# Latent attention: the queries of a head pair made one pair ahead, in output tiles not yet written

## The chip, the core and the metric

The kernel runs on one core of a Trainium2 chip. The core has five engines, each with an instruction stream of its own: TensorE (PE in the profile) multiplies matrices, its weight loads are shown apart as PEld, VectorE (DVE) and ScalarE (ACT) do elementwise work, GpSimd (POOL) helps out, and SyncE (SP) issues transfers from the memory of the chip (HBM). ScalarE issues some transfers too; the profile shows those as ACTq. On-chip data lives in SBUF (128 partitions), sums of matrix products in the banks of PSUM. The metric is the device time of one execution in microseconds (us), lower is better.

## What is computed

Two layers of a decoder trunk with three parallel branches (Mamba-2, latent attention, gated DeltaNet), a merge, an output projection and a feed-forward network, for one sequence of 512 tokens with 1024 channels, in float32. The branch that matters here is the latent attention. Cut to it, the reference is:

```python
def mla_mixer(cq, ckv, k_rope, cos, sin, q_norm_g, w_uq, kv_norm_g, w_ukv):
    H = MLA_HEADS                                  # 8 heads
    q = (rmsnorm(cq, q_norm_g) @ w_uq).reshape(Bsz, S, H, 128 + 64)
    q_nope, q_pe = jnp.split(q, [MLA_NOPE], axis=-1)
    q_pe = apply_rope(q_pe, cos, sin)
    kv = (rmsnorm(ckv, kv_norm_g) @ w_ukv).reshape(Bsz, S, H, 128 + 128)
    k_nope, v = jnp.split(kv, [MLA_NOPE], axis=-1)
    k_pe = apply_rope(k_rope, cos, sin)            # one key for all heads
    sc = (q_nope @ k_nope.T + q_pe @ k_pe.T) * scale, causal
    pr = softmax(sc)
    o = pr @ v
```

Here `cq` has 512 latent channels and `ckv` 256. Each head's query has 128 plain channels and 64 rotary ones.

## The kernel before

**Precision.** Every dense product is made of three matmuls of split numbers, high times high, low times high and high times low (L181, L182, L183 in `mm3`). Weights come from HBM into a raw tile (`wraw`, two buffers), ScalarE rounds the high half (`whi`, L159) and VectorE subtracts it to get the low half (`wlo`, L160); four buffers each of `whi` and `wlo`. The query weights have a split of their own, in four pieces (L552, L553 on ScalarE, L554, L555 on VectorE), because the plain and the rotary channels of a pair of heads are laid apart.

**Order of work.** The program text is a sequence of operations. A planner (the tile framework's scheduler) turns it into one fixed order of instructions for each engine: it goes by the place of an operation in the text, lifted where the text says `high_priority`, by its own costs, and by when buffers come free. So TensorE interleaves work of several steps, and a step's place in the text sets where it may appear, not exactly where. Buffers are rings of tiles with a common tag; a new tile waits until the last reader of the old one is done. What matters here: two raw weight tiles, four accumulator banks (`acc`), three small banks (`sm`) and one output bank (`yt`) in PSUM, eight tiles `mix`, and three tiles each for the plain queries and keys (`qh`, `ql`, `kh`, `kl`).

**Latent attention.** A layer first makes small projections and the latents `cq` and `ck`, with their norms (function `latent`, L500 and L260/L261). Then a loop goes over four pairs of heads, `hp` 0 to 3. For each pair it makes

- the queries: weights (L541 to L556), 36 matmuls of 128x512 (`dense_F`), then `qh`/`ql` for the two heads (L568, L569) and the rotary part `qp` for both (L575). The rotary part goes through `rope`: four transfers issued by ScalarE that exchange its halves (L513), three operations of VectorE (L515 to L517), then two more transfers that swap the heads (L580) and the copies into `qps` and `qpl` (L584, L585, and L586, which reads what the transfers brought). `qpl` is half zero: that half is set once for all pairs (L536);
- the keys: 12 matmuls, `kh`/`kl` (in `head_tiles`, written by `split_act`, L256 and L257);
- the values: 24 matmuls of 128x256, evacuated in eight pieces, by L256 and L257 too. Pairs 0 and 2 have tiles for them; pair 1 writes them into the output tiles `y6` and `y7`, pair 3 into the latent tiles `cq0` and `cq1`, which are not needed any more or not yet;
- for each of the two heads: scores for four blocks of 128 queries (L617 to L619 plain, L620 and L621 rotary, L622 the mask), row maximum (L626, VectorE), exponential (L629, ScalarE), reciprocal and scaling (L630, L631, VectorE), transposes (L639), and the product with the values (L655 to L657), split into the output tiles `y0` to `y7`.

After pair 0 the loop also makes the step sizes of another branch (`step_sizes`). Layer 1 does the loop at about 66 to 195 us of the span, layer 2 at about 1226 to 1358 us. Then a next stage (`ssd_group`) follows, and the planner lets its first matmuls fill gaps in the last pairs.

Of the kernel before, what the change touches and what calls it, by code (L numbers as in the profile page):

```python
# [11 lines left out]
F32R = mybir.dt.float32r  # L12
# [3 lines left out]
ALU = mybir.AluOpType  # L16
# [4 lines left out]
P = 128  # L21
S = 512
# [37 lines left out]
def hybrid_kernel(ctx, tc, a, out, depth=2, taps=None):  # L60
# [4 lines left out]
    def mk(pl, shape, dt, tag, bufs=None):  # L65
        return pl.tile(shape, dt, tag=tag, name=f"{tag}_{next(uid)}", bufs=bufs)
# [5 lines left out]
    def f32(ap):  # L72
        return ap.bitcast(F32)
# [180 lines left out]
    def split_act(hi, lo, src):  # L254
        with tc.high_priority(30):
            act.copy(hi, src)  # L256
            dve.tensor_tensor(lo, src, f32(hi), ALU.subtract)  # L257
# [78 lines left out]
    for ly in range(depth):  # L336
# [34 lines left out]
        ps = sm_bank()  # L371
# [159 lines left out]
        for x in pts:  # L531
            pool.memset(f32(x[:, :P]), 0.0)

        qpl = [mk(ml, [P, S], F32R, f"qpl{j}") for j in range(2)]
        for j in range(2):
            pool.memset(f32(qpl[j][64 * (1 - j) : 64 * (1 - j) + 64]), 0.0)  # L536

        scale = (128 + 64) ** -0.5
        yh, yl = [None] * KD, [None] * KD
        for hp in range(4):  # L540
            def q_weights():  # L541
                for k0 in (0, 2):
                    raw = mk(wp, [P, 768], F32, "wraw", 2)
                    sync.dma_start(raw.rearrange("p (k n) -> p k n", k=2),
                                   a["mla_w_uq"][ly][k0 * P : (k0 + 2) * P, hp * 384 : (hp + 1) * 384].rearrange("(k p) n -> p k n", p=P))
                    for k in range(2):
                        rv = raw[:, k * 384 : (k + 1) * 384].rearrange("p (h n) -> p h n", h=2)
                        hi = mk(wp, [P, 384], F32R, "whi")
# [6 lines left out]
                        dve.tensor_tensor(pv(lo), rv[:, :, P:], f32(pv(hi)), ALU.subtract)  # L555
# [4 lines left out]
            def head_tiles(pss, nm, c=None):  # L560
                res = []
                for ps in pss:
                    hi = mk(ml, [P, S], F32R, nm + "h", 3)
                    lo = mk(ml, [P, S], F32R, nm + "l", 3)
                    if c is None:
                        split_act(hi, lo, ps)
                    else:
                        act.mul(hi, ps, c)  # L568
                        dve.scalar_tensor_tensor(lo, ps, c, f32(hi), ALU.mult, ALU.subtract)  # L569
                    res.append((hi, lo))  # L570
                return res

            qs = head_tiles(pq, "q", scale)
            qp = mk(ml, [P, S], F32, "qp")
            act.mul(qp, pp, scale)  # L575
            qr = rope(qp)

            qd = mk(lp, [P, S], F32, "mix", 8)
            for i in range(2):
                act.dma_start(qd[64 * i : 64 * i + 64], qr[64 * (1 - i) : 64 * (1 - i) + 64])  # L580
            qps = [mk(ml, [P, S], F32R, f"qps{j}") for j in range(2)]
            for j in range(2):
                half, other = (slice(64 * i, 64 * i + 64) for i in (j, 1 - j))
                act.copy(qps[j][half], qr[half])  # L584
                dve.tensor_tensor(qpl[j][half], qr[half], f32(qps[j][half]), ALU.subtract)  # L585
                act.copy(qps[j][other], qd[other])  # L586
            wkv = list(weights(a["mla_w_ukv"][ly], hp * 512, 512, 256))
            with tc.high_priority(30):
                ks = head_tiles(dense_F(wkv, [slice(0, P), slice(256, 256 + P)], 256, ckh, ckl), "k")

            vs = []
            for j in range(2):
                if hp % 2 == 0:
                    v2 = [mk(ml, [P, S], F32R, nm, 2) for nm in ("vh", "vl")]
                elif hp == 1:
                    v2 = [mk(lp, [P, S], F32R, f"y{e}{6 + j}") for e in "hl"]
                else:
                    v2 = [mk(ml, [P, S], F32R, f"cq{e}{j}") for e in "hl"]
                vs.append([x.rearrange("p (t n) -> p t n", t=T) for x in v2])

            def ev(t, ps):
                for j in range(2):
                    split_act(*(x[:, t, :] for x in vs[j]), ps[:, j * P : (j + 1) * P])

            vcols = lambda w: w.rearrange("p (h n) -> p h n", h=2)[:, :, P:]
            dense_T(wkv, 256, 256, ckh, ckl, ev, vcols)

            for j in range(2):
                qh, ql = qs[j]
                kh, kl = ks[j]  # L610
                pn = []
                for t in range(T):
                    n = max(256, (t + 1) * P)
                    tok = slice(t * P, (t + 1) * P)
                    ps = sm_bank()
                    o = ps[:, :n]
                    pe.matmul(o, qh[:, tok], kh[:, :n], start=True, stop=False)  # L617
                    pe.matmul(o, qh[:, tok], kl[:, :n], start=False, stop=False)
                    pe.matmul(o, ql[:, tok], kh[:, :n], start=False, stop=False)  # L619
                    pe.matmul(o, qps[j][:, tok], kps[:, :n], start=False, stop=False)  # L620
# [8 lines left out]
                    act.activation(pt_[:, :n], o, AF.Exp, bias=mx, accum_out=sm)  # L629
                    dve.reciprocal(sm, sm)  # L630
                    dve.tensor_scalar(pt_[:, :n], pt_[:, :n], sm, None, ALU.mult)  # L631
                    pn.append(pt_)
                po = y_bank()
                for kbs in ((0,), (1,), (3, 2)):
                    ps = sm_bank()
                    n = 0
                    for kb in kbs:
                        for t in range(kb, T):
                            pe.transpose(ps[:, n : n + P], pn[t][:, kb * P : (kb + 1) * P], ident)  # L639
                            n += P  # L640
                    if len(kbs) == 1:
                        th = mk(lp, [P, n], F32R, "mix", 8)
                        tl = mk(lp, [P, n], F32R, "mix", 8)
                        split_act(th, tl, ps[:, :n])
                        parts = [(kbs[0], kbs[0] * P, 0)]
                    else:

                        th, tl = pts
                        split_act(th[:, P:], tl[:, P:], ps[:, :n])
                        parts = [(2, 2 * P, 2 * P), (3, 2 * P, 0)]  # L650
                    for kb, c0, c in parts:
                        v_h, v_l = (x[:, kb, :] for x in vs[j])
                        o = po[:, c0:]
                        w = S - c0
                        pe.matmul(o, v_h, th[:, c : c + w], start=kb == 0, stop=False)  # L655
                        pe.matmul(o, v_h, tl[:, c : c + w], start=False, stop=False)
                        pe.matmul(o, v_l, th[:, c : c + w], start=False, stop=kb == T - 1)  # L657
                yh[2 * hp + j], yl[2 * hp + j] = (mk(lp, [P, S], F32R, f"y{e}{2 * hp + j}") for e in "hl")
                split_act(yh[2 * hp + j], yl[2 * hp + j], po)
                tap(f"oT{2 * hp + j}", f32(yh[2 * hp + j]))  # L660
            if hp == 0:
                dec, ndec, beta, dtq, dsk, g24 = step_sizes()
        mp.close()
# [621 lines left out]
```

## Time and profile before

| | |
|---|---|
| time, median of 3 runs | 2350.89 us (2350.47 to 2352.99) |
| time of the profiled execution | 2350.16 us |
| its span | 2348.4 us |
| granted clock of TensorE, mean | 0.999 |
| TensorE busy | 2307.8 us, 98% |
| VectorE busy | 1607.3 us, 68% |
| ScalarE busy | 1154.4 us, 49% |
| GpSimd busy | 58.5 us, 2% |
| moved by transfers | 215.16 MB, 92 GB/s over the span |

How to read the lines that follow. In a timeline a row is: start (us), duration (us), engine, line and operation, output <- input by the program's names, the tile's size, the count, and in brackets how long the engine was idle before it and what ended that idle time. In a list of waits a row is: engine, output and line of the waiting instruction, what it waited for, then the total in us, the number of times, and the longest. Matmuls overlap, so the time that one costs is the distance of two starts, not its duration. Line numbers are those of the kernel before.

### The profile page before, as it was taken

The numbers are of one execution on the slowest core, as the hardware profiler recorded it, in microseconds if no ns is written. First come the engines' busy times: TensorE is split into PE (matmuls) and PEld (weight loads), VectorE is DVE, ScalarE is ACT, GpSimd is POOL, SyncE is SP. The second block draws the span as 40 slices with busy tenths as digits, with TensorE's granted clock in tenths as the row PEclk, the third lists the DMA queues.
The fourth block names the chain that finished last, engine by engine and source line by source line (L and its number), as shares of the span: only waits on it lengthen the run. The fifth ranks groups of instructions, "written<-read, shape, count | busy, mean of one in ns | idle before, by whom it ended". The sixth has DMA issues, their size and how long they took to land.

```text
span 2348.4 us, 32069 instructions
## 1 busy us (share of the span) xinstructions
PE 2307.8 (98%) x11972; PEld 1896.2 (81%) x11972; DVE 1607.3 (68%) x3184; ACT 1154.4 (49%) x2305; POOL 58.5 (2%) x76
## 2 busy tenths in 40 slices
PE   8999999999999999999999999999999999999998
PEld 7787788888887888888887887888887878888886
DVE  6776756775675458767757777667766645677668
ACT  5655434533453345545656553444334534555545
POOL 0000000000000000000000000000000000000000
PEclk9999999999999999999999999999999999999999
DMA  4322232252222443233132222323422224333231
GB/s 131 91 64 72 65 97 70 79 149 73 73 63 72 143 150 102 72 125 117 46 100 78 73 72 70 93 65 106 117 81 66 62 81 161 126 111 105 90 108 45
DMA packets 194172, 215.16 MB, mean 92 GB/s; under 512 B 32352, under 2 KB 153696, under 8 KB 194016
## 3 DMA queue, kind: packets, MB, share of 16 engines
q1 hardware_dynamic: 190496, 207.87, 29.1%
q10 hardware_dynamic: 3520, 5.25, 0.9%
q8 instruction: 94, 1.54, 0.3%
q14 instruction: 62, 0.51, 0.1%
HBM read 200.50 MB, written 7.34 MB: 89 GB/s over the span
## 4 chain that ended last, share of the span: by engine, by line
PE 90%; DVE 5%; DMA 2%; ACT 1%; POOL 1%; issue 1%; SPq 0%; ACTq 0%; DVEq 0%; POOLq 0%
PE acc L181 23%; PE acc L182 23%; PE acc L183 23%; PE sm L183 2%; PE sm L181 2%; PE sm L182 2%; PE sm L735 1%; DVE wlo L160 1%; PE sm L639 1%; PE yt L182 1%; PE yt L181 1%; PE yt L183 1%; PE sm L1000 1%; PE sm L296 1%; PE sm L461 1%
## 5 line engine op out<-in xcount | busy, mean ns | idle before, releaser
L160 DVE TENSOR_TENSOR wlo<-wraw,whi 128x512 fp32r<-128x512 f32 x552 | 377.9, 688 | 401.8 <-ACT whi L159 391.8
L159 ACT CAST whi<-wraw 128x512 fp32r<-128x512 f32 x552 | 341.9, 621 | 623.6 <-PE acc L182 407.9
L181 PE MATMUL acc<-xh,whi 128*128 128x512 f32 (+1 forms) x1184 | 462.0, 391 | 0.0
L182 PE MATMUL acc<-xl,whi 128*128 128x512 f32 (+1 forms) x1184 | 459.4, 388 | 0.0
L183 PE MATMUL acc<-xh,wlo 128*128 128x512 f32 (+1 forms) x1184 | 459.0, 388 | 0.0
L182 PEld LDWEIGHTS acc<-xl,whi 128*128 128x128 f32 x1184 | 223.0, 188 | 42.5 <-issue 1.0
L183 PEld LDWEIGHTS acc<-xh,wlo 128*128 128x128 f32 x1184 | 222.9, 188 | 41.8 <-issue 0.5
L181 PEld LDWEIGHTS acc<-xh,whi 128*128 128x128 f32 x1184 | 222.8, 189 | 41.7 <-issue 0.5
L181 PE MATMUL acc<-yh,whi 128*128 128x512 f32 x384 | 153.1, 402 | 0.0
L182 PE MATMUL acc<-yl,whi 128*128 128x512 f32 x384 | 152.3, 397 | 0.0
L183 PE MATMUL acc<-yh,wlo 128*128 128x512 f32 x384 | 151.4, 394 | 0.0
L183 PE MATMUL acc<-whi,xl 128*128 128x512 f32 (+1 forms) x384 | 144.0, 375 | 0.0
L181 PE MATMUL acc<-whi,xh 128*128 128x512 f32 (+1 forms) x384 | 143.9, 376 | 0.0
L182 PE MATMUL acc<-wlo,xh 128*128 128x512 f32 (+1 forms) x384 | 143.4, 373 | 0.0
L676 DVE SCALAR_TENSOR_TENSOR cva<-acc,pc,cva 128x511 f32<-128x511 f32 (+2 forms) x168 | 120.2, 743 | 16.7 <-ACT cva L672 9.5
L159 ACT CAST whi<-wr 128x512 fp32r<-128x512 f32 x128 | 79.5, 621 | 68.3 <-PE acc L183 32.7
L181 PE MATMUL acc<-whi,yh 128*128 128x512 f32 x256 | 99.7, 390 | 0.0
L183 PE MATMUL acc<-whi,yl 128*128 128x512 f32 x256 | 99.7, 389 | 0.0
L182 PE MATMUL acc<-wlo,yh 128*128 128x512 f32 x256 | 99.6, 389 | 0.0
L160 DVE TENSOR_TENSOR wlo<-wr,whi 128x512 fp32r<-128x512 f32 x128 | 85.8, 685 | 12.6 <-ACT whi L159 12.1
L182 PEld LDWEIGHTS acc<-yl,whi 128*128 128x128 f32 x384 | 72.2, 188 | 16.1 <-issue 1.9
L181 PEld LDWEIGHTS acc<-yh,whi 128*128 128x128 f32 x384 | 71.6, 188 | 16.8 <-ACT yh L260 2.3
(409 smaller groups left out, 4597.9 us busy)
## 6 DMA issues: line engine op xcount, KB each, us to landing
wraw<-in_w_in_dram SPq DMA_DIRECT2D x148, 512.0 KB, 3.6
wraw<-in_w_up_dram SPq DMA_DIRECT2D x64, 512.0 KB, 3.7
wr<-in_w_down_dram SPq DMA_DIRECT2D x32, 1024.0 KB, 5.0
wraw<-in_w_mla_out_dram SPq DMA_DIRECT2D x16, 512.0 KB, 3.4
wraw<-in_w_ssd_out_dram SPq DMA_DIRECT2D x16, 512.0 KB, 3.4
wraw<-in_w_gdn_out_dram SPq DMA_DIRECT2D x16, 512.0 KB, 3.3
wraw<-in_w_out_dram SPq DMA_DIRECT2D x16, 512.0 KB, 3.7
wraw<-in_mla_w_uq_dram SPq DMA_DIRECT2D x16, 384.0 KB, 3.4
```

Source lines behind the costliest of these rows:

```text
L159: act.copy(hi, raw)
L160: dve.tensor_tensor(lo, raw, f32(hi), ALU.subtract)
L181: pe.matmul(o, ah, bh, start=start, stop=False, skip_group_check=more)
L182: pe.matmul(o, ah, bl, start=False, stop=False, skip_group_check=more)
L183: pe.matmul(o, al, bh, start=False, stop=stop, skip_group_check=more)
L296: pe.transpose(ps[:, j * P : (j + 1) * P], xr[j % 2][:, kk * P : (kk + 1) * P], ident)
L461: pe.matmul(ps, w, cum[1][:, t].rearrange("p i l -> p (i l)"), start=True, stop=True)
L639: pe.transpose(ps[:, n : n + P], pn[t][:, kb * P : (kb + 1) * P], ident)
L676: dve.scalar_tensor_tensor(acc[:, d:], ps[:, : S - d], taps_[3 - d], acc[:, d:], ALU.mult, ALU.add)
L735: pe.matmul(py[:, h * 64 : (h + 1) * 64], e2[h // 4][:, h % 4, :], xd[:, h * 64 : (h + 1) * 64], start=True, stop=True)
L1000: pe.matmul(po[:, h * P : (h + 1) * P], pt_[:, h, :], vn[:, h * P : (h + 1) * P], start=True, stop=True)
```

## The change

The loop's body is cut into three functions: `queries(hp)`, `keys(hp)` (which makes keys and values) and `attend(hp, ...)`. The queries of pairs 0 and 1 are made ahead of the loop. In the loop, pair `hp` makes its keys and values and attends, and after that, for `hp` 0 and 1, the queries of pair `hp + 2` are made.

So two pairs' queries are held at once. Even pairs keep the tiles they had. Odd pairs put theirs into tiles that are free at that time: pair 1 its plain queries in the output tiles `y2` and `y3` and its rotary parts in `y4` and `y5`; pair 3 its plain queries in `y6` and `y7` (pair 1's values by then used up) and its rotary parts in the latent tiles `cq2` and `cq3`. The zero halves of the odd pairs' low rotary parts are set anew each time by GpSimd: eight more memsets of 64x512 in the whole program. The number of instructions on the other engines stays.

```diff
-        qpl = [mk(ml, [P, S], F32R, f"qpl{j}") for j in range(2)]
+        base_qpl = [mk(ml, [P, S], F32R, f"qpl{j}") for j in range(2)]
+        clean = lambda x, j: pool.memset(f32(x[64 * (1 - j) : 64 * (1 - j) + 64]), 0.0)
         for j in range(2):
-            pool.memset(f32(qpl[j][64 * (1 - j) : 64 * (1 - j) + 64]), 0.0)
+            clean(base_qpl[j], j)
...
-        for hp in range(4):
+        def head_tiles(pss, nm, c=None, homes=None):
+            res = []
+            for j, ps in enumerate(pss):
+                hi, lo = homes[j] if homes else (mk(ml, [P, S], F32R, nm + e, 3) for e in "hl")
...
+        y_home = lambda k: [mk(lp, [P, S], F32R, f"y{e}{k}") for e in "hl"]
+        cq_home = lambda k: [mk(ml, [P, S], F32R, f"cq{e}{k}") for e in "hl"]
+
+        def queries(hp):
...
-            qs = head_tiles(pq, "q", scale)
+            qs = head_tiles(pq, "q", scale, [y_home(hp * 2 + j if hp == 1 else 6 + j) for j in range(2)] if hp % 2 else None)
...
-            qps = [mk(ml, [P, S], F32R, f"qps{j}") for j in range(2)]
+            if hp % 2:
+                qps, qpl = zip(*((y_home if hp == 1 else cq_home)(k) for k in ((4, 5) if hp == 1 else (2, 3))))
+                for j in range(2):
+                    clean(qpl[j], j)
+            else:
+                qps, qpl = [mk(ml, [P, S], F32R, f"qps{j}") for j in range(2)], base_qpl
...
+            return qs, qps, qpl
+
+        def keys(hp):
...
+            return ks, vs
+
+        def attend(hp, qs, qps, qpl, ks, vs):
...
+        qq = [queries(0), queries(1)]
+        for hp in range(4):
+            attend(hp, *qq[hp], *keys(hp))
+            if hp < 2:
+                qq.append(queries(hp + 2))
             if hp == 0:
                 dec, ndec, beta, dtq, dsk, g24 = step_sizes()
```

More of the change, by code (lines that the diff above doesn't have):

```diff
@@ L532, in hybrid_kernel @@
             pool.memset(f32(x[:, :P]), 0.0)
-        qpl = [mk(ml, [P, S], F32R, f"qpl{j}") for j in range(2)]
+        base_qpl = [mk(ml, [P, S], F32R, f"qpl{j}") for j in range(2)]
+        clean = lambda x, j: pool.memset(f32(x[64 * (1 - j) : 64 * (1 - j) + 64]), 0.0)
         for j in range(2):
-            pool.memset(f32(qpl[j][64 * (1 - j) : 64 * (1 - j) + 64]), 0.0)
+            clean(base_qpl[j], j)
         scale = (128 + 64) ** -0.5
         yh, yl = [None] * KD, [None] * KD
-        for hp in range(4):
+        def head_tiles(pss, nm, c=None, homes=None):
+            res = []
+            for j, ps in enumerate(pss):
+                hi, lo = homes[j] if homes else (mk(ml, [P, S], F32R, nm + e, 3) for e in "hl")
+                if c is None:
+                    split_act(hi, lo, ps)
+                else:
+                    act.mul(hi, ps, c)
+                    dve.scalar_tensor_tensor(lo, ps, c, f32(hi), ALU.mult, ALU.subtract)
+                res.append((hi, lo))
+            return res
+        y_home = lambda k: [mk(lp, [P, S], F32R, f"y{e}{k}") for e in "hl"]
+        cq_home = lambda k: [mk(ml, [P, S], F32R, f"cq{e}{k}") for e in "hl"]
+        def queries(hp):
             def q_weights():
@@ L558, in hybrid_kernel @@
             *pq, pp = dense_F(q_weights(), tiles(384), 512, cqh, cql)
[L560 to L571, printed above, removed]
-            qs = head_tiles(pq, "q", scale)
+            qs = head_tiles(pq, "q", scale, [y_home(hp * 2 + j if hp == 1 else 6 + j) for j in range(2)] if hp % 2 else None)
             qp = mk(ml, [P, S], F32, "qp")
@@ L580, in hybrid_kernel @@
                 act.dma_start(qd[64 * i : 64 * i + 64], qr[64 * (1 - i) : 64 * (1 - i) + 64])
-            qps = [mk(ml, [P, S], F32R, f"qps{j}") for j in range(2)]
+            if hp % 2:
+                qps, qpl = zip(*((y_home if hp == 1 else cq_home)(k) for k in ((4, 5) if hp == 1 else (2, 3))))
+                for j in range(2):
+                    clean(qpl[j], j)
+            else:
+                qps, qpl = [mk(ml, [P, S], F32R, f"qps{j}") for j in range(2)], base_qpl
             for j in range(2):
```

## The prediction

> **What bounds the kernel.** I read the page first, then the waits of TensorE over the whole span, the same waits inside the two stretches of latent attention, and last the timeline around the places where the order changes. The page gives the span and the busy times:
>
> ```profile
> span 2348.4 us, 32069 instructions
> PE 2307.8 (98%) x11972; PEld 1896.2 (81%) x11972; DVE 1607.3 (68%) x3184; ACT 1154.4 (49%) x2305; POOL 58.5 (2%) x76
> ```
>
> TensorE is idle for 2348.4 - 2307.8 = 40.6 us in all. The change leaves its 11,972 instructions as they are, so it can only shorten or lengthen this idle time. The waits of TensorE over the whole span (engine, line, waited for: us in total, times, longest) name what of it concerns the changed stage:
>
> ```profile
> PE sm L620 <- ACT qps L586: 3.2, 3, 1.9
> PE acc L181 <- DVE vl L257: 2.2, 3, 0.8
> ```
>
> L620 is the first matmul of the rotary part of a score, and it waits for the queries' rotary half: that is the wait which a run one pair ahead should remove. Here are the same waits within 58 to 196 us (layer 1) and, below the dots, within 1218 to 1358 us (layer 2):
>
> ```profile
> PE sm L620 <- ACT qps L586: 1.4, 2, 0.8
> PE acc L181 <- DVE vl L257: 0.6, 1, 0.6
> ...
> PE sm L620 <- ACT qps L586: 1.9, 1, 1.9
> PE acc L181 <- DVE vl L257: 1.5, 2, 0.8
> ```
>
> The queries' waits are 1.4 + 1.9 = 3.3 us, the waits for the values' evacuation (which frees an accumulator for the next pair's queries) 0.6 + 1.5 = 2.1 us. What else TensorE waits for there lies in the latents, ahead of the first queries, and does not change. So **at most 5.4 us** can go, 0.23% of the span. The kernel already works ahead: this is the timeline of TensorE in layer 1, pair 0.
>
> ```profile
> 80.19 0.47 PE L181 MATMUL acc<-cqh,whi 128*128 128x512 f32 x1 [0.65 <-DVE vl L257]
> ...
> 80.72 0.39 PE L183 MATMUL acc<-cqh,wlo 128*128 128x512 f32 x1
> 80.96 0.39 PE L181 MATMUL acc<-cqh,whi 128*128 128x512 f32 x1
> ...
> 86.94 0.39 PE L620 MATMUL sm<-kps,qps 128*128 128x256 f32 x1
> ```
>
> Between pair 0's first scores, ended before 80.19, and its rotary part (86.94) the planner has put 27 of the 36 query matmuls of pair 1, as cover for pair 0's rotary chain. Starts a step apart give the cost of a 512-wide matmul as 0.23 us (80.72 to 80.96), so a pair's queries are 36 x 0.2275 = 8.2 us of work that will lie somewhere else.
>
> **The change, part by part.** All of it is order, apart from eight memsets.
>
> *What goes.* Pair 1's queries stand before pair 0's keys, pair 2's after pair 0's first scores, pair 3's after pair 1's. No rotary query is then consumed soon after it is made, and queries no longer queue behind a value's evacuation: **-5.4 us**. Bounds 0 and -5.4.
>
> *Weights of pair 0's keys.* SyncE's ring of two raw buffers now takes both query loads of pair 1 before pair 0's key weights, so these start only when the first query load of pair 1 has been split on VectorE, behind pair 0's own evacuations. The rows of VectorE, then of ScalarE:
>
> ```profile
> 72.69 1.37 DVE L569 SCALAR_TENSOR_TENSOR ql<-acc,qh 128x512 fp32r<-128x512 f32 x2 [1.90 <-ACT qh L568]
> 73.98 0.68 DVE L516 TENSOR_TENSOR mix<-mix,sinT 128x512 f32<-128x512 f32 x1
> 78.76 0.28 DVE L555 TENSOR_TENSOR wlo<-wraw,whi 128x128 fp32r<-128x128 f32 x1
> ...
> 75.41 0.51 ACTq L513 DMA_DIRECT2D mix<-qp  x1
> 76.03 0.53 ACTq L513 DMA_DIRECT2D mix<-qp  x1
> 81.78 0.50 ACTq L580 DMA_DIRECT2D mix<-mix  x1
> 82.74 0.62 ACT L159 CAST whi<-wraw 128x512 fp32r<-128x512 f32 x1 [1.68 <-DMA wraw<-in_mla_w_ukv_dram]
> ```
>
> Now a raw buffer becomes free at 79.04 (78.76 + 0.28) and its key weights can be cast at 82.74: 3.7 us. After the change, pair 0's queries run without pair 0's keys between them, so their evacuation starts some 0.7 us sooner, at 72.0; two of L569 (1.4), L516, L515 and L517 (some 0.65 each as L516 shows), then L554 and L555 (0.5) end at 75.8. With 3.7 and 0.6 for the cast the keys start at 80.1. TensorE gets there sooner: pair 0's last query matmul ends at about 72.5, and 29 matmuls of pair 1 stand before the first key: 72.5 + 29 x 0.2275 = 79.1. So it waits **1.0 us** in each layer. Bounds 0 (the evacuations keep ahead) and 1.8 (they start as late as now).
>
> *Accumulators at the same place.* Three banks hold pair 1's queries and two hold pair 0's keys, of four in all; the values need four. So the second key bank waits for ScalarE's and VectorE's evacuation of pair 1's first query tile, and the values for those of both keys, which in the new order of ScalarE stand behind two issues of L580, two L584 and an L586 that waits for its transfer. The nearest price is the wait for values today, 0.6 to 0.8 us for one bank. Two such waits: **1.5 us** in each layer, bounds 0 and 2.2.
>
> *Softmax behind the rotary chain, pair 0.* This is the largest part. In the new order of ScalarE, the two L586 of pair 1 stand ahead of the exponentials (L629) of the third and the fourth block of pair 0's first head, and L586 waits for a transfer. TensorE's rows for one head's scores, the transfers' times to landing for L580 (first) and L513, and ScalarE's and VectorE's rows for the last block:
>
> ```profile
> 96.36 0.28 PE L617 MATMUL sm<-kh,qh 128*128 128x256 f32 x1
> 100.01 0.39 PE L639 MATMUL sm<-ct,pn 128*128 128x128 f32 x2
> ...
> DMA to landing us min/median/max: 2.2/2.3/5.6
> ...
> DMA to landing us min/median/max: 1.9/2.0/3.9
> ...
> 101.17 0.68 ACT L629 ACTIVATE pn<-sm,mx 128x512 f32<-128x512 f32 x1
> 91.85 0.49 DVE L631 TENSOR_SCALAR pn<-pn,sme 128x512 f32<-128x512 f32 x1
> ```
>
> I count from the end of pair 0's last key matmul. ScalarE evacuates two keys and a query, then the rotary query (L575) until 1.9; four issues of L513 a good 0.6 apart (75.41 to 76.03), the last at 3.8, landed at 5.8 (2.0); L516 and L517 until 7.1; two issues of L580, the second at 7.5, landed at 9.8 (2.3); L586 0.6, the third exponential 0.5, L586 0.6, the fourth 0.7: 12.2, and normalised (0.7 with the reciprocal) at 12.9. TensorE meanwhile has 24 value matmuls at 0.117 (2.8), the scores of the head (100.01 - 96.36 = 3.65) and 21 query matmuls of pair 2 (4.8): 11.2, and then it needs the fourth block's transposes. It waits **1.7 us** in each layer. Bounds 0 (if the chain runs 1.7 us faster) and 3.3, if one transfer lands late: the slowest L580 took 5.6 us, not 2.3, and so great a delay I count by half.
>
> *The same for pair 2.* There the two L586 of pair 3 stand ahead of three of the four exponentials. The chain is the same, with pair 3's rotary query evacuated after the keys again; TensorE has the values (2.8), the scores (3.65), 11 key matmuls (2.5) and a few values of pair 3 for cover: about 2 us less than the chain's 12 to 13. **2.0 us** in each layer, bounds 0 and 3.3. For pair 1 only the first head stands behind L586 and the chain began a whole pair earlier: 0. Pair 3 has no queries behind it: 0.
>
> *Start-up.* The order of the first us of layer 1 changes too. VectorE is to scale the last token block (L291) and split two weights (L160) before it writes the first low half of the normalised input (L261). The rows of VectorE, POOL and TensorE:
>
> ```profile
> 13.25 0.88 DVE L261 SCALAR_TENSOR_TENSOR xl<-sm,pc,xh 128x256 fp32r<-128x256 f32 x2
> 14.04 0.55 DVE L160 TENSOR_TENSOR mix<-wraw,mix 128x384 fp32r<-128x384 f32 x1
> 17.75 0.74 DVE L291 TENSOR_SCALAR xr<-h,nrs 128x1024 f32<-128x1024 f32 x1
> ...
> 13.41 0.55 POOL L265 TENSOR_TENSOR nrs<-nrs,nhalf 128x1 f32<-128x1 f32 x1 [1.12 <-DVE nrs L264]
> 14.31 1.09 POOL L536 MEMSET qpl<- 64x512 f32 x2
> ...
> 14.29 0.41 PE L182 MATMUL yt<-xl,mix 128*96 128x256 f32 x1
> 18.39 0.63 PE L182 MATMUL acc<-wlo,xh 128*128 128x512 f32 x1
> 18.81 0.52 PE L183 MATMUL acc<-whi,xl 128*128 128x512 f32 x1
> 19.40 0.39 PE L182 MATMUL acc<-wlo,xh 128*128 128x512 f32 x1
> 25.30 0.93 PE L296 MATMUL sm<-ct,xr 128*128 128x128 f32 x7
> ```
>
> L291 needs POOL's factor, there at 13.96. So L291 until 14.7, L160 until 15.2, L261 until 15.7: the matmul now at 14.29 starts at about 15.8, 1.5 us later. TensorE has nothing else ready there, but the last token block is scaled 3 us sooner, so that part comes back until the transposes of 25.30. I take **+1.0 us**, bounds 0 and 2.7. A matmul costs 0.42 us here until about 18.8 (18.39 to 18.81) and 0.23 us from 19.17 on. [...]
>
> *Memsets.* Eight more halves at about 0.55 us (two take 1.09), 2.2 us of POOL in each layer. POOL is busy for 58.5 us of the span; in layer 1 two come before its first factor, at which it has idled, and two stand with nothing behind them that is due. 0 us, bounds 0 and 0.5 in layer 2, where two stand between the factors of the norm.
>
> *The sum.* Per layer 1.0 + 1.5 + 1.7 + 2.0 = 6.2 us, for two layers 12.4; less 5.4; with 1.0 at the start: +8.0 us. The profiled execution took 2350.16 us, which gives 2358.2; it lies 0.7 us below the median of the runs, 2350.89, so that I round to **2358 us**.
>
> **The rivals.**
> - *It works as named.* ScalarE reaches L586 after its transfers have landed, as it does for 13 of 16 of them now, and the 5.4 us go: 2350.2 - 5.4 + 1.0 at start-up = 2346. For it: the 3.3 us of waits are real and on the path. Against it: nothing more is to be had in these stages, and the new order puts more behind L586 than now.
>
> ```profile
>   DMA mix<-mix: 2.1, 3
> ```
>
>   That row is ScalarE's idle time before L586, in total and times. Chance 0.15.
> - *One wait for another.* The change moves waits and neither gains nor loses: keys and accumulators cost their 2.5 us a layer and the exponentials nothing, 5.0 + 1.0 - 5.4 = +0.6: 2351. For it: the cover on TensorE is near 1.7 us of what is wanted, so a small error decides. Chance 0.22. This holds also for the case that it does not do what it says, since 27 of 36 query matmuls run ahead already.
> - *Much slower.* [...] Chance 0.15.
>
> **How the numbers follow.** My forecast (2355.6 to 2364) has 0.48. A measurement of this kernel can tell about 0.2%, 4.7 us, from no change. Faster by more needs less than 2346.2: half of the first rival and its neighbours, 0.13. Within 0.2%, 2346.2 to 2355.6: the rest of it and the second rival, 0.22. Slower: 0.65. The range leaves out one in ten on each side: 2346 to 2368. If the signs are taken apart, the likeliest case has 2354 to 2364.
>
> **What would show it.** In the changed profile: no wait of L620 for L586 in either stage; a new wait of L181 for ScalarE's L159 or its weights' transfer at about 79 us; waits of L639 for L631 at pairs 0 and 2; ScalarE idle before L586 by more than 2.1 us in all; the matmul of 14.29 at 15.8. If ScalarE's idle time before L586 stays at 2 us, or L639 does not wait, the main part of my sum is wrong and the time is the first or second rival's. If TensorE's order outside these stages differs, none of this holds.

## The result, and the profile after

The changed kernel takes 2362.2 us (2361.56 to 2364.0, 5 runs) against 2351.02 us for the kernel before: a ratio of 1.0047, 95% interval 1.0034 to 1.0060. It is slower by 11.2 us. The profiled execution took 2361.98 us. Its page begins:

```profile
span 2360.2 us, 32061 instructions
PE 2311.8 (98%) x11972; PEld 1895.3 (80%) x11972; DVE 1607.6 (68%) x3184; ACT 1154.4 (49%) x2305; POOL 63.3 (3%) x84
```

TensorE has the same 11,972 instructions. The waits of TensorE over the whole span (engine, output and line, waited for: us in total, times, longest) have new rows. Lines are now those of the changed kernel: L635 is the first matmul of a score (L617 before), L647 the exponential (L629), L572 the rounding of query weights (L552), L574 their split (L554), L550 the low half of a query (L569), L595 and L597 the copies of a rotary query (L584, L586), L657 the transposes (L639).

```profile
PE acc L181 <- DVE vl L257: 3.6, 4, 1.0
PE sm L635 <- ACT kh L256: 2.9, 2, 1.5
PE sm L635 <- ACT pn L647: 1.3, 2, 0.7
PE acc L181 <- ACT whi L159: 1.2, 2, 0.7
PE acc L183 <- DVE wlo L574: 1.2, 2, 0.6
```

The wait for the rotary queries (3.2 us before) is gone from the list. Others have come or grown. The five above are the largest of them in latent attention; together they are 10.2 us, where the values' evacuation alone stood for 2.2 us before.

**Where the time went.** The same instructions can be found in both timelines ahead of, between and behind the two stages of latent attention. The kernel before:

```profile
58.35 0.28 PE L183 MATMUL acc<-whi,xl 128*128 128x256 f32 x1
223.83 0.39 PE L183 MATMUL acc<-whi,xl 128*128 128x512 f32 x1
1222.27 0.96 PE L181 MATMUL acc<-cqh,whi 128*128 128x512 f32 x3 [0.29 <-ACT cqh L260]
1385.95 0.39 PE L183 MATMUL acc<-whi,xl 128*128 128x512 f32 x1
```

and the changed kernel:

```profile
59.34 0.28 PE L183 MATMUL acc<-whi,xl 128*128 128x256 f32 x1
229.95 0.48 PE L183 MATMUL acc<-whi,xl 128*128 128x512 f32 x1
1228.92 0.96 PE L181 MATMUL acc<-cqh,whi 128*128 128x512 f32 x3 [0.29 <-ACT cqh L260]
1396.87 0.48 PE L183 MATMUL acc<-whi,xl 128*128 128x512 f32 x1
```

The distance of the two is 1.0 us at 58 us, 6.1 us after the first stage, 6.65 us before the second, 10.9 us after it, and 11.8 us at the end (the spans, 2360.2 and 2348.4). So the first stage lost 5.1 us, the second 4.3 us, the start 1.0 us (although its input came 1.4 us sooner, see below), and 1.4 us came in stages whose order is the same in both kernels; such steps differ between profiles, in one of the runs below by 3.0 us.

**The new waits in the order of time**, layer 1, timeline of TensorE (in brackets: idle before, and what ended it):

```profile
78.26 0.50 PE L181 MATMUL acc<-cqh,whi 128*128 128x512 f32 x1 [0.46 <-ACT whi L572]
...
80.65 0.39 PE L182 MATMUL acc<-cql,whi 128*128 128x512 f32 x1
81.51 0.50 PE L181 MATMUL acc<-ckh,whi 128*128 128x512 f32 x1 [0.47 <-ACT whi L159]
81.84 0.39 PE L183 MATMUL acc<-cqh,wlo 128*128 128x512 f32 x1
...
84.20 0.50 PE L181 MATMUL acc<-ckh,whi 128*128 128x512 f32 x1 [0.36 <-DVE yl L550]
88.22 0.68 PE L635 MATMUL sm<-kh,qh 128*128 128x256 f32 x3 [1.45 <-ACT kh L256]
94.89 0.50 PE L635 MATMUL sm<-kh,qh 128*128 128x512 f32 x1 [0.67 <-ACT pn L647]
98.74 0.96 PE L183 MATMUL acc<-cqh,wlo 128*128 128x512 f32 x3 [0.60 <-DVE wlo L574]
155.63 0.50 PE L181 MATMUL acc<-ckh,whi 128*128 128x512 f32 x1 [0.98 <-DVE vl L257]
158.07 0.50 PE L181 MATMUL acc<-ckh,whi 128*128 128x512 f32 x1 [0.79 <-DVE vl L257]
```

Six waits stand at pair 0 (pair 1's query weights, which are now made there, pair 0's key weights, an accumulator, its keys' evacuation, the softmax of its first head, pair 2's query weights) and two at the accumulators of pair 3's keys, which the values of pair 2 still hold. The rows from 80.65 to 81.84 show something besides. From 80.65 to 81.51 are 0.86 us; a matmul takes 0.23, so 0.63 us were lost where 0.47 are listed, and the next start comes 0.33 us later instead of 0.23. **So this wait costs about 0.26 us more than its row says.** Of that, 0.16 us lie in how the row counts: its idle time begins at the listed end of the matmul before, 0.39 us after that one's start, while without a wait the next would start after 0.23. The other 0.10 us are a slower start after the wait. For five other waits (at 80.19 in the kernel before, and at 84.20, 94.89, 155.63 and 158.07 here) the same sum gives 0.23 to 0.31 us.

What delayed the keys can be read off SyncE (the load of the key weights), VectorE (the split ahead of it) and ScalarE, in this order:

```profile
76.76 0.37 SPq L172 DMA_DIRECT2D wraw<-in_mla_w_ukv_dram  x1
...
76.45 0.28 DVE L575 TENSOR_TENSOR wlo<-wraw,whi 128x128 fp32r<-128x128 f32 x1
...
80.83 1.14 ACT L159 CAST whi<-wraw 128x512 fp32r<-128x512 f32 x2 [1.93 <-DMA wraw<-in_mla_w_ukv_dram]
87.07 0.62 ACT L597 CAST qps<-mix 64x512 fp32r<-64x512 f32 x1 [1.03 <-DMA mix<-mix]
87.59 0.57 ACT L256 CAST kh<-acc 128x512 fp32r<-128x512 f32 x1
...
88.83 0.58 ACT L256 CAST kh<-acc 128x512 fp32r<-128x512 f32 x1
```

The load starts when VectorE has split the last of pair 1's first raw tile, 76.73, and is cast 4.1 us later. The last key matmul started at 86.38, yet ScalarE evacuates the two heads' keys at 87.59 and 88.83, since one L597 stands before each of them (at 87.07 and 88.19), the first of which waited 1.03 us for its transfer.

### The profile page after: what moved, and what is told of

The parts are those of the page before. It is cut to its first block, busy times and chain, and to the rows that moved or that the text cites. A ratio compares the mean times of both kernels' runs of the same rounds, so it can differ in the third digit from the quotient of the medians.

```text
span 2360.2 us, 32061 instructions
## 1 busy us (share of the span) xinstructions
PE 2311.8 (98%) x11972; PEld 1895.3 (80%) x11972; DVE 1607.6 (68%) x3184; ACT 1154.4 (49%) x2305; POOL 63.3 (3%) x84
## 4 chain that ended last, share of the span: by engine, by line
PE 89%; DVE 6%; ACT 2%; DMA 2%; issue 1%; POOL 1%; SPq 0%; ACTq 0%; DVEq 0%; POOLq 0%
PE acc L181 22%; PE acc L183 22%; PE acc L182 22%; PE sm L183 2%; PE sm L181 2%; PE sm L182 2%; PE sm L759 1%; DVE wlo L160 1%; PE sm L657 1%; PE yt L182 1%; PE yt L183 1%; PE yt L181 1%; PE sm L1024 1%; PE sm L461 1%; PE yt L673 1%
```

## The experiments

All keep the reference's computation; they only change orders and places. Each was measured beside the kernel before, and the ratios are to that. Line numbers differ by a few between them.

### 1. The start: startup_order and zero_on_vector

The odd pairs' zero halves made late by GpSimd, so that nothing new stands first in its queue:

```diff
                 for j in range(2):
-                    clean(qpl[j], j)
+                    z = slice(64 * (1 - j), 64 * (1 - j) + 64)
+                    pool.tensor_tensor(qpl[j][z], kpe[z], kpe[z], ALU.subtract)
```

> The changed kernel, but the odd pairs' zero halves are made by GpSimd as the rotary key minus itself, so that they cannot come first in its queue. TensorE's, ScalarE's, VectorE's and SyncE's orders in latent attention are then the same as in the changed kernel, and the order of the first 25 us is that of the kernel before. My theory: the two early memsets alone turned the start-up order, which cost 1.0 us by the trace (the transposes of the second half start at 26.29 instead of 25.30, even though the input came earlier): 1 to 2.5 us below the changed kernel, about 2360.5. Rival: the start-up shift is chance of the input's transfers, and the run equals the changed kernel, 2362.

Measured: 2362.59 us, ratio 1.0050 (1.0036 to 1.0064). No gain. In its trace the start was as in the kernel before, but the two stages then lost more, 6.2 and 5.2 us. One cause in the first is in the rows of GpSimd and, below the dots, of VectorE:

```profile
75.37 2.20 POOL L591 TENSOR_TENSOR yl<-mix 64x512 fp32r<-64x512 f32 x2 [9.57 <-DVE mix L517]
...
75.48 1.13 DVE L575 TENSOR_TENSOR wlo<-wraw,whi 128x128 fp32r<-128x128 f32 x1
76.91 1.22 DVE L528 TENSOR_TENSOR kps<-mix,kph 64x512 fp32r<-64x512 f32 x1 [0.30 <-ACT kph L526]
```

The split L575 took 1.13 us instead of 0.28, and L528 1.22 instead of 0.69, while GpSimd subtracted (0.28 and 0.69 are their times in zero_on_vector, below, without the subtraction). L575 is the instruction that frees the raw tile for the keys' weights. (Another part is a transfer: the first rotary copy waited 1.60 us for it here, 1.03 us in the changed kernel.) A memset of the changed kernel shows no such thing, though it overlaps for 0.23 us only: beside the one at 1183 us two splits took 1.29 us, and the next two, at 1186 us with none beside them, 1.29 us as well. So a second run set pair 1's zero halves of layer 1 by VectorE, at a time when it idles:

```diff
-                    clean(qpl[j], j)
+                    if ly or hp == 3:
+                        clean(qpl[j], j)
+                    else:
+                        dve.memset(f32(qpl[j][64 * (1 - j) : 64 * (1 - j) + 64]), 0.0)
```

> The changed kernel, but in layer 1 pair 1's two zero halves are set by VectorE instead of GpSimd. The start-up order is then that of the kernel before, and latent attention's order that of the changed kernel, with no long GpSimd operation next to VectorE's rotary products. My theory: in the run startup_order the gain at the start (1.3 us by the trace) was lost again because GpSimd's subtraction slowed VectorE at 75 to 78 us (1.13 us for a split that takes 0.28 otherwise), which held back the raw tile of pair 0's keys. So this run lies 1 us below the changed kernel: 2361. Rival: the loss in startup_order was chance of the transfers and has nothing to do with GpSimd: 2362.5 again.

Measured: 2361.86 us, ratio 1.0048 (1.0035 to 1.0061). The changed kernel has 1.0047, so the start's order is worth less than these runs can tell. Its input also arrived at another time in every profile (first transpose at 8.85 us in the changed kernel, 10.25 before, 11.88 here), by more than the step in question. All further kernels but three (keys0_first, only_pair1_ahead, pair1_after_pair0, which have GpSimd's subtraction) are built on this one.

### 2. Pair 0: own_raw_for_keys0, rotary_copies_after_keys0, and both

Pair 0's key weights loaded into two free output tiles instead of the ring:

```diff
-            wkv = list(weights(a["mla_w_ukv"][ly], hp * 512, 512, 256))
+            def own_raw():
+                for k in range(2):
+                    raw = mk(lp, [P, 512], F32R, f"y{'hl'[k]}6")
+                    sync.dma_start(f32(raw), a["mla_w_ukv"][ly][k * P : (k + 1) * P, :512])
+                    hi, lo = split_half(f32(raw))
+                    yield k, hi.unsqueeze(1), lo.unsqueeze(1)
+
+            wkv = list(weights(a["mla_w_ukv"][ly], hp * 512, 512, 256) if hp else own_raw())
```

> As zero_on_vector, but pair 0's key weights are loaded into two output tiles that are free then, so that they do not wait for a place in the ring of raw tiles. My theory: this takes the waits for the key weights and the bank next to them (0.5 to 0.7 + 0.4 us and restarts), but the evacuation of the keys behind the rotary chain stays: 0.7 to 1.3 us a layer less than zero_on_vector, 2358.5 to 2360. Rival: the late weights are the root of all waits at pair 0, since everything after them starts later: 3 us a layer less, 2355.

Measured: 2354.23 us, ratio 1.0012 (1.0004 to 1.0021): 7.6 us less than zero_on_vector, more than the waits for the weights alone. My theory was too small, and the time is nearly the rival's. The waits of TensorE in 58 to 215 us, without those that all kernels share (here L645 is a score, L657 the exponential, L659 the scaling, L667 a transpose):

```profile
PE sm L645 <- ACT kh L256: 1.7, 1, 1.7
PE sm L645 <- ACT pn L657: 1.6, 2, 0.9
PE acc L181 <- DVE vl L257: 1.4, 1, 1.4
PE sm L667 <- DVE pn L659: 0.8, 1, 0.8
```

The rows for key weights, for the accumulator and for pair 2's query weights are gone: 0.8 + 0.2 + 0.6 us in zero_on_vector, each with its restart, and part of the values' wait (0.3 us for pair 1's query weights remain). But the waits for the keys and for the exponentials, which the rival wanted gone too, are still there and longer, and one at the transposes of pair 2 is new. In layer 1 the lists add up to 8.3 us here and 8.1 in zero_on_vector, so the listed waits do not show where the gain lies. The order of later pairs changed too, since the planner laid them out anew, so the 7.6 us are not the ring's alone. Moving the copies of the rotary queries behind the keys, without early weights:

```diff
-            for j in range(2):
+            def rest():
+                for j in range(2):
...
+            if hp:
+                rest()
+            else:
+                held.append(rest)
             return qs, qps, qpl
...
                 ks = head_tiles(dense_F(wkv, [slice(0, P), slice(256, 256 + P)], 256, ckh, ckl), "k")
+            if held:
+                held.pop()()
```

> As zero_on_vector, but the copies of pair 0's rotary queries, which wait for their transfers, stand behind pair 0's keys in the program, so that ScalarE evacuates the keys first. The key weights still come late. My theory: the wait of the first scores for the keys (1.5 us a layer) goes, and with it some of the delay of the exponentials behind it; the rotary scores wait instead, but later, behind 24 value matmuls: 1 to 1.5 us a layer less than zero_on_vector, 2358 to 2359. Rival: the chain is only moved, its wait comes back at the rotary scores: 2361.

Measured: 2362.43 us, ratio 1.0046 (1.0032 to 1.0059): nothing gained. The wait moved, as the rival had it, though not to the rotary scores that it named. The wait for the keys is gone, and came back as these two, at the weights of later queries and at a bank that an exponential has not yet read:

```profile
91.98 0.50 PE L181 MATMUL acc<-cqh,whi 128*128 128x512 f32 x1 [0.93 <-ACT whi L574]
95.07 0.80 PE L647 MATMUL sm<-kh,qh 128*128 128x512 f32 x1 [1.90 <-ACT pn L659]
```

ScalarE does the copies now behind the keys and ahead of pair 0's exponentials. Both cures together:

> The two cures of pair 0 together: pair 0's key weights in tiles of their own, and the copies of its rotary queries behind its keys. My theory, after the runs so far: with the weights early the wait of the first scores for the keys (1.7 and 1.6 us) was what was left of pair 0; with the copies behind the keys it goes too, and nothing before pair 2 is late: 2 to 3 us under own_raw_for_keys0, 2351 to 2352, with the values' wait at pair 3's keys (about 1 + 1 us a layer) still there. Rival: as in rotary_copies_after_keys0 the wait only moves (there the fourth block of scores waited 1.9 us for an exponential), and the time stays at 2354.

Measured: 2353.42 us, ratio 1.0008 (0.9999 to 1.0018), not to be told from the kernel before. Waits in 58 to 215 us (L654 is a score, L666 the exponential):

```profile
PE acc L181 <- DVE vl L257: 1.8, 2, 1.0
PE sm L654 <- ACT pn L666: 0.8, 1, 0.8
PE acc L181 <- ACT whi L574: 0.7, 1, 0.7
```

Pair 0 keeps two waits, 1.5 us together (the second and third row), and the two at pair 3's keys are the largest that is left, as expected. With early weights the copies behind the keys did no harm, presumably because the chain had more time. By the medians, 8.4 us go with the two cures (2361.86 less 2353.42) and 7.6 us with the early weights alone. The instructions of the section on where the time went leave out the start and all other stages: between the first and the second of them, and between the third and the fourth, zero_on_vector lost 5.0 and 3.7 us against the kernel before, own_raw_for_keys0 2.8 and 0.4, both cures 2.0 and 0.2. An estimate tells how much of that is lost early. Take the time since the first of these instructions (the third in layer 2), and subtract what the matmuls done since then cost by their width, 0.23 us at 512. When 30 us of matmuls are done, at about 100 and 1267 us, in the softmax of pair 0, zero_on_vector and the changed kernel are 4.0 to 4.4 us behind the kernel before in each layer, own_raw_for_keys0 2.3 and 1.8, both cures about half a us. **So some 8 of the change's 11 us are lost at pair 0. Loading its key weights early, which the change had queued behind pair 1's queries, takes back about half of them there, and 5.5 us over the two stages** (the new layout of the later pairs included; 7.6 us in the medians).

### 3. Keys before the run ahead: keys0_first and keys0_first_vector

```diff
-        qq = [queries(0), queries(1)]
+        qq = [queries(0)]
+        kv = [keys(0)]
+        qq.append(queries(1))
         for hp in range(4):
-            attend(hp, *qq[hp], *keys(hp))
+            attend(hp, *qq[hp], *(kv[0] if hp == 0 else keys(hp)))
```

> As startup_order, but pair 0's keys and values are made before pair 1's queries; all else is one pair ahead. SyncE's ring then loads pair 0's key weights before pair 1's query weights, and pair 0's keys are evacuated ahead of its rotary chain. My theory: this takes away the late key weights, the bank and the key evacuation behind the chain (0.5 + 0.4 + 1.5 us and restarts, 2.5 to 3 us a layer): 2353 to 2356. Rival: the order on the ring does not matter, any order that holds two pairs' queries costs as much: 2360.

> As zero_on_vector, but pair 0's keys and values before pair 1's queries. My theory: the run keys0_first without GpSimd's subtraction, which there delayed the keys' low half (a wait of 0.5 us) and the values' evacuation (0.9 instead of 0.7): 1 us a layer less, 2352. Rival, the subtraction costs nothing there: 2354.

Measured: keys0_first 2354.2 us, ratio 1.0016 (1.0007 to 1.0025); keys0_first_vector 2351.39 us, ratio 1.0003 (0.9995 to 1.0012). The first, with GpSimd's subtraction, waits for the keys' low half and longer for the values, among others; the second does not. keys0_first (two rows), then keys0_first_vector:

```profile
77.96 0.39 PE L181 MATMUL acc<-whi,ckh 128*128 128x256 f32 x1 [0.46 <-DVE kl L257]
80.74 0.47 PE L181 MATMUL acc<-cqh,whi 128*128 128x512 f32 x1 [0.91 <-DVE vl L257]
```

```profile
80.47 0.47 PE L181 MATMUL acc<-cqh,whi 128*128 128x512 f32 x1 [0.65 <-DVE vl L257]
151.87 0.50 PE L181 MATMUL acc<-ckh,whi 128*128 128x512 f32 x1 [1.19 <-DVE vl L257]
```

Two pairs' queries are held here as in the changed kernel, and the waits for rotary queries are gone, yet the time is that of the kernel before. zero_on_vector, which differs from keys0_first_vector in this edit alone, took 10.5 us more. The order at pair 0 was therefore the cause of the loss, and holding two pairs was not. In the two stages keys0_first_vector is ahead of the kernel before by no more than 0.4 us each. In layer 1 the rotary waits that went had 1.35 us listed, and the waits at pair 3's keys that came, at 151.87 above all, 1.42 us; I take this for the reason that nothing is gained.

### 4. Which part of the run ahead: four more orders

Only pair 1 ahead, with pairs 2 and 3 in their old places (`if hp > 1: qq.append(queries(hp))` at the head of the loop), and pair 1's queries after pair 0's attention:

> As startup_order, but only pair 1's queries are made ahead (before pair 0's keys); those of pairs 2 and 3 stand before their own keys as in the kernel before. My theory: most of the cost is at pair 0 (waits of 0.5 + 0.5 + 0.4 + 1.5 + 0.7 + 0.6 us in layer 1, each with some 0.2 us for the restart), so it keeps 3 to 4 us a layer over the kernel before: 2357 to 2359. Rival: the cost lies with pairs 2 and 3 (the values' evacuation behind pair 3's rotary products, 1.0 + 0.8 us), and the time is within 2 us of the kernel before, 2351 to 2353.

> As startup_order, but pair 0 is made and attended first, as in the kernel before, and the queries of pairs 1 and 2 follow it; those of pair 3 come one pair ahead. My theory: without the cost at pair 0 what stays is that of pairs 2 and 3, some 2.5 us a layer with restarts, less the waits for the rotary queries and the values that are gone, about 1 to 2 us a layer: 2351 to 2354. Rival: pairs 2 and 3 carry the cost, and the time is 2357 or more.

Measured: only_pair1_ahead 2367.7 us, ratio 1.0074 (1.0061 to 1.0087); pair1_after_pair0 2360.47 us, ratio 1.0046 (1.0033 to 1.0058). Both are slower than I expected, and the first is the slowest order of all. It lies 5.1 us above startup_order, from which it differs in this order alone. So pairs 2 and 3 ahead do not cost there, they help. Two rows of only_pair1_ahead tell why:

```profile
102.94 0.77 PE L658 MATMUL sm<-ct,pn 128*128 128x128 f32 x5 [0.88 <-DVE pn L650]
151.99 0.39 PE L639 MATMUL sm<-kps,qps 128*128 128x256 f32 x1 [1.67 <-ACT qps L598]
```

The transposes of pair 0's softmax (L658) have no query matmuls of pair 2 beside them any more and wait for its scaling, and pair 2's rotary scores wait again, 1.67 us where it was 0.78 in the kernel before. In pair1_after_pair0 pair 0 loses little (1 us), but pair 1's keys, scores and values find nothing prepared and wait five times. Two more, on top of keys0_first_vector: pair 3 in its old place (`if hp == 0: qq.append(queries(2))`, `if hp == 2: qq.append(queries(3))`), and pairs 2 and 3 both in place:

> As keys0_first_vector, but pair 3's queries stand before pair 3's keys, as in the kernel before; only those of pairs 1 and 2 come ahead. My theory: what keeps keys0_first_vector from a gain is the pair 2 to 3 boundary, where the value evacuation of pair 2 stands behind pair 3's rotary chain (waits of 0.23 + 1.19 + 0.18 us in layer 1, 0.23 + 1.19 + 0.48 in layer 2, each with a restart). Without it 2 us a layer go: 2347 to 2348. Rival: another place takes over (pair 3's own rotary scores, 2 us), and it stays at 2351.

> As keys0_first_vector, but only pair 1's queries come ahead; pairs 2 and 3 are in place. My theory: the order is then nearly that of the kernel before, pair 1's queries being the cover of pair 0's rotary chain in both, but pair 0's softmax has only keys and values of pair 1 as cover, and pair 2's rotary wait is back: 2351 to 2353. Rival: the gain comes from pair 1 alone, and the time is that of keys0_first_pair3_in_place.

Measured: keys0_first_pair3_in_place 2354.39 us, ratio 1.0014 (1.0005 to 1.0023); keys0_first_only_pair1 2359.91 us, ratio 1.0034 (1.0021 to 1.0048). The wait at pair 3's keys went, and others took its place. The two longest in layer 1 of keys0_first_pair3_in_place are at the product of pair 0's softmax with the values, and at a matmul of the next stage, whose accumulator the values of pair 3 still hold:

```profile
103.01 0.50 PE L676 MATMUL yt<-mix,vh 128*128 128x512 f32 x1 [1.36 <-ACT mix L256]
169.98 0.47 PE L181 MATMUL acc<-xh,whi 128*128 128x512 f32 x1 [1.64 <-DVE cql L257]
```

My theory failed here. The last order makes keys and values first and the next pair's queries second, in every pair:

```diff
-        qq = [queries(0), queries(1)]
+        qq = [queries(0)]
         for hp in range(4):
-            attend(hp, *qq[hp], *keys(hp))
-            if hp < 2:
-                qq.append(queries(hp + 2))
+            kv = keys(hp)
+            if hp < 3:
+                qq.append(queries(hp + 1))
+            attend(hp, *qq[hp], *kv)
```

> As zero_on_vector, but in every pair the keys and values come first, then the next pair's queries, then the attention. So key weights precede the next query weights on the ring at every pair. Theory one, the ring decides: all late key weights are gone and the removed waits show, 2347 to 2349. Theory two, cover decides: the planner pulls each pair's keys and values into the softmax of the pair before, where queries were the cover, and they wait there for weights and evacuations, as in keys0_first_only_pair1: 2355 to 2360.

Measured: 2365.91 us, ratio 1.0057 (1.0043 to 1.0072), slower than either theory had it, on the side of theory two. Its two largest new waits of layer 1, in 58 to 215 us:

```profile
PE yt L676 <- ACT mix L256: 4.3, 3, 2.8
PE acc L181 <- DVE kl L257: 2.8, 3, 1.3
```

The planner pulls the keys and values into the softmax of the pair before, and they need ScalarE and VectorE just when the softmax does. Query matmuls are longer, 0.23 us each against 0.12 for a value, and their results are wanted late, so they are the better cover, and a pair has only 36 of them. That is how I read these rows; no run changes the cover alone.

No order tried beat the kernel before.

## Why the prediction was right, point by point

The direction was right, and the size: forecast +8.0 us, measured +11.2, within the range. In part this was luck: 3.7 of the 6.2 us a layer were put at the transposes, which wait 0.18 us in each layer; other waits behind the same rotary chain came to nearly the same sum. By its steps:

- **What goes.** Right for the rotary queries: L620's wait is gone. Of the values' waits, that of layer 1 and one of layer 2 went; another of layer 2 came back as 0.50 us for an output tile.
- **Weights of pair 0's keys.** The mechanism as forecast; forecast 1.0 us, measured 0.47 and 0.74 listed, 0.7 and 1.0 with the restart. But the step was taken too narrowly: early weights took 7.6 us from the time (5.5 in the two stages). The waits that went from the list are 1.6 us a layer, 2.3 with their restarts; the keys behind the rotary copies and the softmax waited longer than before, so how the rest comes about stays open. A wait for pair 1's own query weights, 0.46 us at 78.26 in layer 1, stands in no term.
- **Accumulators at the same place.** Forecast 1.5 us a layer; measured 0.36 + 1.45 in layer 1. The keys' evacuation behind L586 was the larger part, and the first scores waited for it, not the values, as the forecast had it.
- **Softmax behind the rotary chain, pair 0.** Forecast 1.7 us, at the transposes. This place was wrong: the transposes did not wait, presumably because pair 2's queries were cover enough once TensorE itself was late. Instead the fourth block's scores waited 0.67 us for a bank that the first exponential had not yet read, and pair 2's query weights 0.60 us for VectorE. The sum, 1.3 us, is close; the step is named wrongly.
- **Pair 2.** Forecast 2.0 us, again at the transposes; measured 0.98 + 0.79 + 0.18 us, and the first two at the accumulators for pair 3's keys. The reason is VectorE's order. For the first wait, the evacuations of the values stand behind a row maximum that VectorE had waited 1.92 us for, the split of pair 3's key weights (1.28 us) and pair 3's rotary products; for the second, behind two more row maxima (1.14 us) and the low half of a rotary query (0.67 us). So the same chain has a part in it, though not the only one.

```profile
151.89 0.29 DVE L644 TENSOR_REDUCE mx<-sm 128x1 f32<-128x128 f32 x1 [1.92 <-PE sm L640]
...
153.30 0.68 DVE L516 TENSOR_TENSOR mix<-mix,sinT 128x512 f32<-128x512 f32 x1
153.90 0.28 DVE L257 TENSOR_TENSOR vl<-acc,vh 128x128 fp32r<-128x128 f32 x1
154.10 0.68 DVE L517 TENSOR_TENSOR mix<-mix,mix 128x512 f32<-128x512 f32 x1
```

- **Start-up.** Forecast +1.0 us with a wait of 1.5 us. The wait is there:

```profile
15.19 0.53 PE L182 MATMUL yt<-xl,mix 128*96 128x256 f32 x1 [1.80 <-DVE xl L261]
...
20.40 0.28 PE L182 MATMUL yt<-xl,mix 128*96 128x256 f32 x1
20.52 0.28 PE L183 MATMUL yt<-xh,mix 128*96 128x256 f32 x1
```

  It was hidden in part by an input that came 1.4 us sooner. Counted from the first transpose (10.25 us before, 8.85 after), the transposes of the second half come after 15.05 us before and after 17.44 us in the changed kernel (25.30 and 26.29): 2.4 us lost, where 1.0 was forecast. The twelve other orders, which lack this wait, need 14.4 to 15.6 us. Whether the early input was chance the profiles don't show; in the time of the runs the start could not be told from nothing (zero_on_vector).

  The upper bound of 2.7 us holds 1.7 us more than the 1.0 taken, and no run shows these 1.7 us. What the runs show is a step in the cost of matmuls at the start: a 256-wide one in the changed kernel costs 0.21 us at 20.01 to 20.22 and 0.12 us at 20.40 to 20.52, a 512-wide one in the kernel before 0.42 us at 18.39 to 18.81 and 0.23 us at 19.17 to 19.40. The granted clock reads 1.00 from 8 to 30 us in both, so the step shows in the spacings alone. It comes 11.6 us after the first transpose in the changed kernel, 8.9 us after it in the kernel before, and 7.2 to 10.0 us after it in the twelve orders without the gap at 15 us. So it lies later where the gap is, but it also differs by 2.8 us among orders without it, and that the gap moved it was not shown.
- **Memsets.** No row shows a cost of their own, as forecast: the first two run at 0.97 us, where GpSimd idles. But they are what turned the order of the start, which is the old one again in startup_order and zero_on_vector, where GpSimd does not set these halves first.
- **What the sum left out.** What a wait costs beyond its row: the first stage lists twelve waits where it listed seven, and the second eleven for six, some 1.3 us each at 0.26 a wait. The lists themselves are 4.0 and 2.5 us longer than before. Together that is 5.3 and 3.8 us, near the 5.1 and 4.3 that the two stages lost; the forecast had 3.5 a layer (6.2 less 2.7).
- **The signs named beforehand.** I had said that without a wait of L639, and with ScalarE's idle time before L586 at 2 us or less, the main part of the sum would be wrong. Both came (1.7 us idle, 0.18 us at the transposes), so by its own signs the main part of the sum was wrong as named. The time was slower all the same: the waits sat at other steps of the chain than those where I looked.

The rival "one wait for another" described orders that the change did not choose: keys0_first_vector and own_raw_and_copies_after_keys0 are such trades.

## What to carry to other kernels

Before work is moved ahead, look at what shares its queues: here the loads of one pair's queries went ahead of another pair's keys on a ring of two raw tiles (TensorE waited 0.47 us for the weights), and copies that wait for a transfer, 1.03 us here, went ahead of evacuations in ScalarE's fixed order. Cover is a stock, not a free good: matmuls taken from one wait leave another bare (0.88 us at the transposes of pair 0 in only_pair1_ahead), so count for each wait which matmuls remain beside it. When waits are summed, add the restart of each, some 0.26 us here, to what its row lists.

## What the runs showed of the hardware that I had not expected

- A wait of TensorE cost about 0.26 us beyond the listed idle time (80.65 to 81.84 above: 1.19 us for two matmuls of 0.23 and a listed 0.47; 0.23 to 0.31 us at five other waits). 0.16 us of it come from where the row begins to count.
- Beside GpSimd subtractions of 64x512 (two in 2.20 us, startup_order) a VectorE split took 1.13 us, without them 0.28 us (zero_on_vector). Beside a GpSimd memset of the same size, which overlapped for 0.23 us, two larger splits took 1.29 us, as two did with none beside them (the changed kernel, 1183 and 1186 us). Whether the subtraction alone makes the 2.8 us between keys0_first and keys0_first_vector isn't settled, as the two ran on different chips and their later waits differ too.
